# Attention turns: the weighted sums read in halves, one PSUM copy moved ahead of an exponential, weight rounding on another engine, and a new order at the end

## The chip, the cores and the metric

The kernel runs on one core of one Trainium2 chip. TensorE (PE) multiplies, VectorE (DVE), ScalarE (ACT) and GpSimd (POOL) work element by element, SyncE's queue (SP) issues most transfers. Each engine takes its instructions in the order in which the program wrote them for it; between engines, semaphores keep the order that the data need. The metric is the device time of one execution in microseconds, as the median of several runs.

## The reference

One encoder layer on 1024 positions of 1024 channels, in float32:

```
h = rms_norm(x, norm1_g);  z = h @ w_in
a, gate, q, k, v = split(z)
conv_out = silu(layer_norm(depthwise_conv(a * sigmoid(gate))))
q, k = rms_norm per head;  attn_out = neighbourhood_attention(q, k, v, rpb)
x = x + concat(conv_out, attn_out) @ w_out
h = rms_norm(x, norm2_g)
x = x + (silu(h @ w_gate) * (h @ w_up)) @ w_down
```

The attention has 8 heads of 64 channels on a grid of 16 rows by 64 columns. Each query sees a window of 8 rows by 16 columns, clamped inside the grid, with a learned bias per offset, a softmax over the window, and a weighted sum of the values. The change lies in this part and just behind it.

## The kernel before

Matrices are multiplied in two rounded parts: a value is rounded ("hi", `fp32r`), the rest ("lo") is the value minus hi, and `mac` adds three products (L122 to L126). `split` (L114) makes both parts: ScalarE casts, another engine subtracts.

The attention is cut into 8 sets, listed in `order` (L720): a half of the grid's rows (`rh`) by one of four column blocks (`cb`). A set has 128 queries and 253 to 372 keys; it has four pairs of heads. Index `i` counts all 32 pairs, `i // 4` is the set and `i % 4` the pair. For one pair:

- `score_mm(i)` (L732): TensorE makes the scores of two heads, each in a PSUM bank of its own.
- `score_max` (L746): VectorE adds the bias table, writes to SBUF tile `e`, and takes the maximum of each row. The table of a set comes by one large transfer (`table`, L668).
- `score_exp` (L761): ScalarE takes the exponential and its sum; `score_norm` (L770): VectorE inverts the sums, GpSimd scales `e`.
- `flip(i)` (L777): TensorE transposes the weights into two banks; `flip_out(i, r, eng)` (L787) copies bank `r` to SBUF, on ScalarE unless VectorE is named.
- `weigh(i)` (L795): TensorE multiplies the values with the weights and sums into `o`, one PSUM tile of 128x512 for each set, a quarter for each pair. There are two such tiles at a time.
- `evac_hi` (L817, ScalarE) and `evac_lo` (L822, VectorE) read the whole tile of a finished set as hi and lo parts.

The value rows that `weigh` reads come by `load_vw` (L693), eight or more small transfers for each column block, issued by SP. Each transfer signals on one of eight lanes, and a lane's next transfer is not issued before the last one has landed.

The PSUM banks come from three tags: `mm` with four, `tp` with two (`o` lies there), `cx` with two. Scores and flips of odd pairs take `mm`, of even pairs `cx`, in turn. So the scores of pair i (even) go to the two banks that the flip of pair i-2 filled in the turn before, and have to wait until both `flip_out`s have read them; the flip of i-2 in the same turn then takes the banks that the scores of i filled.

The order of the work is written out by hand: `manual_schedule` keeps it (L78). The loop at L964 makes one turn for two pairs, i = 4, 6, ... 30, and within a turn the steps of different pairs interleave: TensorE does scores of i+1, flip of i-3, scores of i, weighing of i-5 and i-4, flip of i-2. Turns 14 to 28 each also prepare a quarter of a weight tile of the output projection (`take_parts`, L173; one of `jobs` each turn): ScalarE casts 128x256, GpSimd subtracts.

Behind the loop (L997 to L1026) stands its end: the last flips and weighings, `fill` (first products of the output projection for the channels that are finished; its first call also loads ScalarE's square-root table), `sum_split` and `conv_mean`, the mean of the convolution channels as a product with ones. Then the projection runs.

Of the kernel before, what the change touches and what calls it, by code (L numbers as in the profile page):

```python
# [6 lines left out]
F32 = mybir.dt.float32  # L7
F32R = mybir.dt.float32r
AF = mybir.ActivationFunctionType
OP = mybir.AluOpType  # L10
# [61 lines left out]
def build(ctx, tc, a):  # L72
# [41 lines left out]
    def split(hi, lo, src, sub=(pool,), cast=True):  # L114
        if cast:
            act.copy(hi, src)  # L116
        n = src.shape[-1] // len(sub)
        for i, eng in enumerate(sub):
            sl = slice(i * n, (i + 1) * n)
            eng.tensor_tensor(*[w[..., sl] for w in (lo, src, hi.bitcast(F32))], OP.subtract)  # L120
# [22 lines left out]
    chunks, raws = [], {}  # L143
# [29 lines left out]
    def take_parts(jobs, n=4, sub=pool):  # L173
        i = pos[1]
        hi, lo = chunks[i][2]()
        w = 1024 // n
        if i == 0:
            dve.tensor_copy(hi[:, :w], raws[i][:, :w])

        def part(o):  # L180
            sl = slice(o, o + w)
            split(hi[:, sl], lo[:, sl], raws[i][:, sl], (sub,), i + o > 0)
            if o + w == 1024:
                raws.pop(i)
                issue()
        pos[1] += 1
        jobs.extend(lambda o=o: part(o) for o in range(0, 1024, w))
# [480 lines left out]
    def table(rh, ty):  # L668
        n = AR[rh] * NCOL[ty]
        src = tf[rh, ty].rearrange("j i h c -> (j i) (h c)")  # L670
        if rh == 0 and ty == 0:
            parts = [(G(f"tab{k}")[:, :4 * n], 4 * k) for k in range(2)]
        else:
            parts = [(H(f"tab{rh}{ty}")[:, :NH * n], 0)]
        heads = []
        for w, h0 in parts:
            nc.sync.dma_start(w, src[:, h0 * n:h0 * n + w.shape[-1]])
            heads += [w[:, o:o + n] for o in range(0, w.shape[-1], n)]
        return heads
# [13 lines left out]
    def load_vw(cb, *gs):  # L693
        c0, ncol = WIN[cb]
        if (cb, gs[0] // 2) not in vwt:
            vwt[cb, gs[0] // 2] = G(f"vw{cb}{gs[0]}").rearrange("p (g d) -> p g d", d=512)
        w = vwt[cb, gs[0] // 2]
        v4 = vd.rearrange("(g r c) d -> r c g d", r=4, c=GW)
        for r in range(4):
            value_rows(w, r * ncol, slice(gs[0] % 2, gs[-1] % 2 + 1), v4[r, c0:c0 + ncol, gs[0]:gs[-1] + 1, :], ncol)  # L700
        n = whole(4 * ncol)
        if n > 4 * ncol:
            nc.sync.dma_start(w[4 * ncol:n, gs[0] % 2:gs[-1] % 2 + 1, :], zd[:n - 4 * ncol, :len(gs), :])
        for g in gs:
            vw[cb, g] = w[:, g % 2, :]
# [59 lines left out]
    def both(i, s):  # L765
        for hh in range(2):
            score_max(i, hh, s)
            score_exp(i, hh)

    def score_norm(i):  # L770
        rs = sums.pop(i)
        dve.reciprocal(rs, rs)  # L772
        for hh in range(2):
            pool.tensor_scalar(es[i][:, hh], es[i][:, hh], rs[:, hh:hh + 1], 1.0, op0=OP.mult, op1=OP.mult)  # L774


    def flip(i):  # L777
        pp[i] = [(mm if i % 2 else cx)(f"p{i}{r}") for r in range(2)]
        gs = groups(i // 4)
        m = whole(gs[0].stop)  # L780
        for hh in range(2):
            for g, k in enumerate(gs):
                for r, pt in enumerate(pp[i]):
                    q, o = slice(r * 64, r * 64 + 64), (hh * len(gs) + g) * 64
                    pe.transpose(pt[:m, o:o + 64], et[i][q, hh, k.start:k.start + m], ident[q, q])  # L785

    def flip_out(i, r, eng=None):  # L787
        gs = groups(i // 4)
        m, n = whole(gs[0].stop), len(gs) * P
        w = et[i].rearrange("p h n -> p (h n)")[:m, :2 * n].rearrange("p (r n) -> p r n", r=2)  # L790
        v = w.rearrange("p r (h g q) -> p r h g q", h=2, q=64)
        pTs[i] = [v[:, :, h] for h in range(2)]
        (eng.tensor_copy if eng else act.copy)(w[:, r], pp[i][r][:m, :n])  # L793
# [19 lines left out]
    def at_of(s_):  # L813
        rh, cb = order[s_]
        return [w[:, :, cb * P:cb * P + P] for w in at[rh]]

    def evac_hi(s_):  # L817
        if not at:
            at.extend(half(f"at{h}") for h in range(2))
        act.copy(at_of(s_)[0], os_[s_])  # L820

    def evac_lo(s_):  # L822
        hi, lo = at_of(s_)
        dve.tensor_tensor(lo, os_[s_], hi.bitcast(F32), OP.subtract)

    def value(t):
        z = nat(2, t, mm if t < 6 else tp)
# [4 lines left out]
    def load_window(cb):  # L832
        load_vw(cb, 0, 1)
        load_vw(cb, 2, 3)
# [34 lines left out]
    flip_out(0, 1, dve)  # L869
    step()  # L870
    load_vw(0, 3)
    tab[1, 3] = table(1, 2)
    load_window(3)


    xd = dr.tile([KB, P, S], F32, name="xd")
# [21 lines left out]
    def conv_mean(h):  # L898
        cw["m", h] = tp(f"mr{h}")
        for n, w in enumerate(cr[:2]):  # L900
            pe.matmul(cw["m", h], cr[2], w[:, h * 512:(h + 1) * 512], start=n == 0, stop=n == 1)
# [23 lines left out]
    def conv_var(h):  # L925
        pt = tp(f"vs{h}")
        cw["v", h] = SM(f"cv{h}", 4)
        column_rstd(cw["v", h], pt, cw["s", h], DC)
# [35 lines left out]
    for i in range(4, 32, 2):  # L964
        if i == 4:
            tab[0, 1] = tab[0, 2] = table(0, 1)
        if i == 8:
            tab[1, 1] = tab[1, 2] = table(1, 1)
        if i in (8, 12):
            load_window(i // 6)  # L970
        if i in (14, 22):
            take_parts(jobs)
        sc = score_mm(i + 1)
        if i == 4:
            score_norm(3)
        else:
            flip(i - 3)
        sa = score_mm(i)
        flip_out(i - 3, 0)
        both(i + 1, sc)  # L980
        both(i, sa)
        flip_out(i - 3, 1, dve)
        score_norm(i + 1)
        if i > 4:
            weigh(i - 5)
        weigh(i - 4)
        flip(i - 2)
        flip_out(i - 2, 0)
        flip_out(i - 2, 1, dve)
        score_norm(i)  # L990
        if i % 4 == 0 and i > 4:
            evac_hi(i // 4 - 2)
        if i % 4 == 2 and i > 6:
            evac_lo(i // 4 - 2)
        if jobs:
            jobs.pop(0)()
    fill(0, 4, 5)  # L997
    sum_split(0)
    flip(29)
    flip_out(29, 0)  # L1000
    flip_out(29, 1)
    flip(30)
    flip_out(30, 0)
    flip_out(30, 1, dve)
    weigh(27)
    weigh(28)
    evac_hi(6)
    fill(0, 6, 7)
    flip(31)
    flip_out(31, 0)  # L1010
    flip_out(31, 1)
    evac_lo(6)
    sum_split(1)
    conv_mean(0)
    fill(1, 4, 5, 6, 7)
    conv_dev(0)

    cm += [half(f"cm{h}") for h in range(2)]
    slots = {0: lambda: ([weigh(i) for i in (29, 30, 31)], evac_hi(7), evac_lo(7)), 3: lambda: conv_var(0),
             4: lambda: (conv_mean(1), conv_dev(1)), 6: lambda: (conv_rows(0), conv_norm(0, 0)), 12: lambda: conv_var(1),  # L1020
             18: lambda: conv_rows(1),
             19: lambda: (act.activation(warm, eps, AF.Silu), [conv_norm(0, c) for c in (1, 2, 3)],
# [596 lines left out]
```

## Time and profile before

| What | Value |
|---|---|
| Median of 3 runs | 1013.18 us (1012.17 to 1014.35) |
| The profiled execution, its own time | 1013.09 us |
| Its span on the core | 1011.4 us |
| TensorE clock granted | 1.00 of full speed |
| TensorE busy | 1005.3 us (99%) |
| VectorE, ScalarE, GpSimd busy | 781.5, 477.6, 456.5 us |
| 230 to 287 us, the attention turns: TensorE, VectorE, ScalarE, GpSimd busy | 55.6, 45.2, 51.0, 39.8 us |
| 287 to 297 us, their end | 9.7, 5.8, 9.1, 5.6 us |

A row of the timeline gives the start in us from the span's start, the duration in us, the engine, the line, the operation, what is written from what is read (names of tiles, `o<-e,vw`), the shape, how many instructions were merged, and in brackets how long the engine sat idle before it and what ended that. TensorE records a float32 product as two instructions, so a weighing of two pairs is 24 rows, the scores of a pair are 4, and a flip is 12. The chain of waits goes back from the last instruction, at each step to what released it.

### The profile page before, as it was taken

To read this page: it belongs to the slowest core of one execution; us is meant where nothing else is said; L and a number is where in the kernel's file an instruction comes from. 1 tells how busy PE (TensorE), PEld (TensorE's weight loads), DVE (VectorE), ACT (ScalarE), POOL (GpSimd) and SP (SyncE) were. 2 spreads that over 40 slices of the span, in tenths; PEclk is the share of its full clock that TensorE was granted. 3 is DMA by queue.
4 is the path that set the end of the run, shared out by engine and by line. 5 is a ranking of instruction groups with operands and counts; after the bars stand their busy time and mean duration, and the time that the engine had idled before them with its cause. 6 is when DMAs were issued, how large, how long until landed. Compare 5 with 4: busy or idle time off the path is not lost.

```text
span 1011.4 us, 15446 instructions
## 1 busy us (share of the span) xinstructions
PE 1005.3 (99%) x5442; PEld 841.1 (83%) x5442; DVE 781.5 (77%) x1242; ACT 477.6 (47%) x1044; POOL 456.5 (45%) x385
## 2 busy tenths in 40 slices
PE   9999999999999999999999999999999999999998
PEld 7888888886788888888888888888888888888887
DVE  5788997896869376987877778778778766768874
ACT  7556357837987245532443333333433453443432
POOL 1036674535763375274655666566665100003300
PEclk9999999999999999999999999999999999999999
DMA  9416782235524520224343343433441796634631
GB/s 343 180 47 219 210 239 90 90 111 187 173 83 172 202 85 21 76 103 156 120 151 125 134 139 125 148 130 118 156 135 44 279 363 222 207 105 131 222 115 42
DMA packets 75757, 151.72 MB, mean 150 GB/s; under 512 B 14472, under 2 KB 23560, under 8 KB 75040
## 3 DMA queue, kind: packets, MB, share of 16 engines
q1 hardware_dynamic: 73664, 147.20, 43.1%
q10 hardware_dynamic: 2016, 3.54, 1.0%
q8 instruction: 43, 0.70, 0.3%
q14 instruction: 34, 0.28, 0.1%
HBM read 112.07 MB, written 44.11 MB: 154 GB/s over the span
## 4 chain that ended last, share of the span: by engine, by line
PE 93%; DVE 3%; DMA 2%; POOL 1%; ACT 0%; SPq 0%; issue 0%; DVEq 0%; ACTq 0%
PE B L124 6%; PE B L125 6%; PE B L126 6%; PE D L124 4%; PE D L125 4%; PE D L126 4%; PE pj L124 3%; PE z L125 3%; PE z L126 3%; PE pj L126 3%; PE pj L125 3%; PE gl L124 3%; PE gl L126 3%; PE gl L125 3%; PE z L124 3%; DVE cv L388 3%
## 5 line engine op out<-in xcount | busy, mean ns | idle before, releaser
L388 DVE SCALAR_TENSOR_TENSOR cv<-u,par,cv 128x1009 f32<-128x1009 f32 (+14 forms) x92 | 117.4, 1277 | 2.3
L1562 POOL TENSOR_TENSOR ou<-ou,resm 128x512 f32<-128x512 f32 x8 | 12.5, 1562 | 140.2 <-DVE ou L1553 126.5
L415 POOL TENSOR_TENSOR pa<-pa,pr 128x1022 f32<-128x1022 f32 (+5 forms) x24 | 58.0, 2418 | 38.1 <-ACT pr L414 37.6
L116 ACT CAST op<-sr 128x512 fp32r<-128x512 f32 x77 | 47.6, 619 | 56.8 <-PE B3d L126 26.4
L120 DVE TENSOR_TENSOR op<-sr,op 128x512 fp32r<-128x512 f32 x77 | 57.8, 751 | 17.0 <-ACT op L116 16.8
L116 ACT CAST op<-wd 128x512 fp32r<-128x512 f32 x54 | 33.4, 619 | 29.4 <-DVE wd L1457 18.3
L1110 DVE TENSOR_TENSOR ts<-gu,ts 128x512 f32<-128x512 f32 x36 | 40.5, 1126 | 0.6
L120 DVE TENSOR_TENSOR op<-wd,op 128x512 fp32r<-128x512 f32 x54 | 39.1, 724 | 2.4 <-ACT op L116 1.3
L774 POOL TENSOR_SCALAR e<-e,rs 128x341 f32<-128x341 f32 (+5 forms) x64 | 32.8, 528 | 17.2 <-DVE rs L772 14.8
L763 ACT ACTIVATE e<-e,mx 128x341 f32<-128x341 f32 (+5 forms) x64 | 34.9, 550 | 10.9 <-DVE mx L758 10.7
L1371 DVE TENSOR_TENSOR g<-D,g 128x512 f32<-128x512 f32 x22 | 15.2, 689 | 24.0 <-PE D L126 24.0
L442 ACT ACTIVATE sq<-z,r 128x64 f32<-128x64 f32 x96 | 28.3, 328 | 5.9 <-PE z L126 5.9
L758 DVE CUSTOM_DVE_ANT_0 e<-s,tab 128x341 f32<-128x341 f32 (+5 forms) x64 | 27.6, 479 | 3.4 <-PE s L741 3.0
L1348 ACT ACTIVATE D<-D 128x512 f32<-128x512 f32 x22 | 12.8, 582 | 36.5 <-DVE D L1347 36.5
L414 ACT ACTIVATE pr<-u,par 128x1022 f32<-128x1022 f32 (+5 forms) x24 | 27.0, 1138 | 1.6 <-ACT vs L472 1.6
L1064 POOL TENSOR_TENSOR sq<-sq,sq 128x512 f32<-128x512 f32 x12 | 17.6, 1464 | 16.5 <-ACT sq L1060 16.2
L741 PE MATMUL s<-kT,qT 64*128 64x341 f32 (+5 forms) x128 | 24.3, 458 | 0.4 <-ACT e L793 0.4
L806 PEld LDWEIGHTS o<-e,vw 128*64 128x64 f32 (+1 forms) x336 | 18.1, 136 | 6.4 <-issue 6.2
L806 PE MATMUL o<-e,vw 128*64 128x128 f32 (+1 forms) x336 | 21.9, 277 | 0.7 <-DMA vw<-vd 0.5
L793 DVE COPY e<-p 128x384 f32<-128x384 f32 (+2 forms) x30 | 16.1, 536 | 8.0 <-PE p L785 7.3
L1060 ACT ACTIVATE sq<-xT 128x512 f32<-128x512 f32 x16 | 10.0, 632 | 25.3 <-DVE xT L954 25.2
L954 DVE TENSOR_TENSOR xT<-pj,xT 128x512 f32<-128x512 f32 x16 | 10.7, 681 | 14.3 <-PE pj L126 14.3
(1502 smaller groups left out, 3785.9 us busy)
## 6 DMA issues: line engine op xcount, KB each, us to landing
gu<-in_gu SPq DMA_DIRECT2D x44, 512.0 KB
sr<-sd SPq DMA_DIRECT2D x77, 256.0 KB
sd<-sd SPq DMA_DIRECT2D x22, 512.0 KB
wd<-in_wd SPq DMA_DIRECT2D x36, 256.0 KB
sd<-g SPq DMA_DIRECT2D x33, 256.0 KB
x<-in_x SPq DMA_DIRECT2D x8, 512.0 KB
xT<-in_xp SPq DMA_DIRECT2D x8, 512.0 KB
xd<-xT SPq DMA_DIRECT2D x16, 256.0 KB
```

The source lines that it names most:

```text
L116: act.copy(hi, src)
L120: eng.tensor_tensor(*[w[..., sl] for w in (lo, src, hi.bitcast(F32))], OP.subtract)
L124: pe.matmul(acc, lh, rh, start=start, stop=False, skip_group_check=True)
L125: pe.matmul(acc, lh, rl, start=False, stop=False, skip_group_check=True)
L126: pe.matmul(acc, ll, rh, start=False, stop=stop, skip_group_check=True)
L388: dve.scalar_tensor_tensor(acc[:, o], uc[:, i], dwk[:, c, t:t + 1], acc[:, o], OP.mult, OP.add)
L415: pool.tensor_tensor(pa[:, o], pa[:, o], pr[:, o], OP.add)
L442: act.activation(sq[:, h * HD:(h + 1) * HD], z[:, h * HD:(h + 1) * HD], AF.Square, scale=r, accum_out=ss[:, h:h + 1])
L763: act.activation(e, e, AF.Exp, bias=mx.pop((i, hh)), scale=-1.0, accum_out=sums[i][:, hh:hh + 1])
L774: pool.tensor_scalar(es[i][:, hh], es[i][:, hh], rs[:, hh:hh + 1], 1.0, op0=OP.mult, op1=OP.mult)
L806: pe.matmul(os_[s_][hh * HD:(hh + 1) * HD, hp], v[:n, c:c + HD], pTs[i][hh][:n, :, g], start=g == 0, stop=g == len(gs) - 1)
L1110: (pool if (i, n) in ON_POOL else dve).tensor_tensor(o, l, r, OP.subtract)
```

## The change

- The finished sums are no longer read as a whole set. `evac` reads a slice of the pairs, and `evac_half(i)` reads the two pairs that end with pair i. In turn i the hi half of pairs up to i-5 is read at the turn's end, and the lo half of pairs up to i-7 ahead of the weighing.
- In the turn, `flip_out(i-2, 0)` now stands ahead of `score_exp(i, 1)` on ScalarE. `score_norm(i)` moves from the turn's end into the next turn, behind the first maximum.
- In `take_parts` with GpSimd, VectorE makes the hi part in place of ScalarE.
- The transfer of one bias table is issued between the two halves of a block's value rows, where it stood ahead of both.
- The end of the loop is written in another order: flip 29 first, then `fill`, the weighing of 27 and 28, flips 31 and 30, and `conv_mean(0)` ahead of the second `sum_split`.

```
@@ take_parts
         def part(o):
             sl = slice(o, o + w)
-            split(hi[:, sl], lo[:, sl], raws[i][:, sl], (sub,), i + o > 0)
+            if sub is pool:
+                dve.tensor_copy(hi[:, sl], raws[i][:, sl])
+            split(hi[:, sl], lo[:, sl], raws[i][:, sl], (sub,), sub is not pool and i + o > 0)
@@ reading of the sums
-    def evac_hi(s_):
+    def evac(s_, lo=False, ks=slice(0, 4)):
         if not at:
             at.extend(half(f"at{h}") for h in range(2))
-        act.copy(at_of(s_)[0], os_[s_])
-
-    def evac_lo(s_):
-        hi, lo = at_of(s_)
-        dve.tensor_tensor(lo, os_[s_], hi.bitcast(F32), OP.subtract)
+        h, l = [w[:, ks] for w in at_of(s_)]
+        if lo:
+            dve.tensor_tensor(l, os_[s_][:, ks], h.bitcast(F32), OP.subtract)
+        else:
+            act.copy(h, os_[s_][:, ks])
+
+    def evac_half(i, lo=False):
+        evac(i // 4, lo, slice(i % 4 - 1, i % 4 + 1))
@@ transfers ahead of the loop
     load_vw(0, 3)
+    load_vw(3, 0, 1)
     tab[1, 3] = table(1, 2)
-    load_window(3)
+    load_vw(3, 2, 3)
@@ a turn
         sc = score_mm(i + 1)
-        if i == 4:
-            score_norm(3)
-        else:
+        if i > 4:
             flip(i - 3)
         sa = score_mm(i)
         flip_out(i - 3, 0)
-        both(i + 1, sc)
-        both(i, sa)
+        score_max(i + 1, 0, sc)
+        score_norm(i - 2 if i > 4 else 3)
+        score_max(i + 1, 1, sc)
+        score_exp(i + 1, 0)
+        score_exp(i + 1, 1)
+        score_max(i, 0, sa)
+        score_max(i, 1, sa)
+        score_exp(i, 0)
         flip_out(i - 3, 1, dve)
         score_norm(i + 1)
+        if i > 6:
+            evac_half(i - 7, True)
+        if jobs:
+            jobs.pop(0)()
         if i > 4:
             weigh(i - 5)
         weigh(i - 4)
         flip(i - 2)
         flip_out(i - 2, 0)
         flip_out(i - 2, 1, dve)
-        score_norm(i)
-        if i % 4 == 0 and i > 4:
-            evac_hi(i // 4 - 2)
-        if i % 4 == 2 and i > 6:
-            evac_lo(i // 4 - 2)
-        if jobs:
-            jobs.pop(0)()
+        score_exp(i, 1)
+        if i > 4:
+            evac_half(i - 5)
@@ behind the loop
+    flip(29)
+    flip_out(29, 0)
+    score_norm(30)
+    evac_half(25, True)
+    flip_out(29, 1, dve)
     fill(0, 4, 5)
     sum_split(0)
-    flip(29)
-    flip_out(29, 0)
-    flip_out(29, 1)
-    flip(30)
-    flip_out(30, 0)
-    flip_out(30, 1, dve)
     weigh(27)
     weigh(28)
-    evac_hi(6)
+    evac_half(27)
+    evac_half(27, True)
+    for i in (31, 30):
+        flip(i)
+        flip_out(i, 0)
+        flip_out(i, 1, dve)
     fill(0, 6, 7)
-    flip(31)
-    flip_out(31, 0)
-    flip_out(31, 1)
-    evac_lo(6)
+    conv_mean(0)
     sum_split(1)
-    conv_mean(0)
     fill(1, 4, 5, 6, 7)
     conv_dev(0)
...
-    slots = {0: lambda: ([weigh(i) for i in (29, 30, 31)], evac_hi(7), evac_lo(7)), 3: lambda: conv_var(0),
+    slots = {0: lambda: ([weigh(i) for i in (29, 30, 31)], evac(7), evac(7, True)), 3: lambda: conv_var(0),
```

## The prediction, on record before the changed kernel was run

> **What bounds the kernel now.** First the head of the page, for the span; TensorE is busy throughout, and its clock is granted in full (both in the table above).
>
> ```profile
> span 1011.4 us, 15446 instructions
> ```
>
> A busy TensorE says little here, because the ends of matmuls are modelled and touch; what counts is how far apart the starts lie. The change touches the attention turns (about 236 to 286 us) and the tail behind them (to 297). Behind that TensorE runs projections back to back, so I let a shift at 297 pass to the end in full. So I read next the chain of waits in that stage, then TensorE's timeline in its early and middle turns.
>
> ```profile
> 240.81 5.36 DMA tab<-tf
> 246.18 5.60 DMA vw<-vd
> ```
>
> ```profile
> 237.96 0.73 PE L785 MATMUL p<-ident,e 64*128 64x64 f32 x8 [0.31 <-DVE mx L758]
> ...
> 239.83 0.73 PE L741 MATMUL s<-kT,qT 64*128 64x276 f32 x4 [0.37 <-ACT e L793]
> ...
> 250.06 1.31 PE L806 MATMUL o<-e,vw 96*64 96x128 f32 x20
> 251.92 0.44 PE L806 MATMUL o<-e,vw 96*64 96x128 f32 x4 [0.55 <-DMA vw<-vd]
> 252.29 0.54 PE L785 MATMUL p<-ident,e 64*96 64x64 f32 x12
> ...
> 255.72 0.54 PE L785 MATMUL p<-ident,e 64*96 64x64 f32 x12
> ...
> 256.72 0.50 PE L785 MATMUL p<-ident,e 64*96 64x64 f32 x12
> 257.06 0.79 PE L741 MATMUL s<-kT,qT 64*128 64x341 f32 x4
> 257.78 1.53 PE L806 MATMUL o<-e,vw 96*64 96x128 f32 x24
> 259.24 0.69 PE L785 MATMUL p<-ident,e 64*96 64x64 f32 x12
> ...
> 263.14 0.59 PE L785 MATMUL p<-ident,e 64*128 64x64 f32 x12
> ...
> 265.52 1.89 PE L806 MATMUL o<-e,vw 96*64 96x128 f32 x24
> 267.34 0.59 PE L785 MATMUL p<-ident,e 64*128 64x64 f32 x12
> ```
>
> The early turns end on transfers: the table of 1152 KB, then the value rows behind it, for which the weighing at 250.06 stands still. Undisturbed, 24 products take 257.78 to 259.24, 1.46; here 252.29 - 250.06 = 2.23, so 0.77 is lost. At 265.52 it is 1.82, so 0.36 is lost.
>
> Now one late turn (i = 28, rows 372 wide) on three engines, by their timelines.
>
> ```profile
> 278.53 0.58 PE L785 MATMUL p<-ident,e 64*128 64x64 f32 x12
> 278.95 0.84 PE L741 MATMUL s<-kT,qT 64*128 64x372 f32 x4
> 279.63 0.54 PE L785 MATMUL p<-ident,e 64*128 64x64 f32 x12
> 280.08 0.90 PE L741 MATMUL s<-kT,qT 64*128 64x372 f32 x4
> 280.90 1.53 PE L806 MATMUL o<-e,vw 128*64 128x128 f32 x24
> 282.37 0.59 PE L785 MATMUL p<-ident,e 64*128 64x64 f32 x12
> ...
> 286.19 0.59 PE L785 MATMUL p<-ident,e 64*128 64x64 f32 x12
> ```
>
> ```profile
> 279.55 0.47 ACT L793 COPY e<-p 128x384 f32<-128x384 f32 x1
> 279.91 0.42 ACT L116 CAST wo06h<-wo06r 128x256 fp32r<-128x256 f32 x1
> ...
> 281.02 0.60 ACT L763 ACTIVATE e<-e,mx 128x372 f32<-128x372 f32 x1 [0.32 <-DVE mx L758]
> ```
>
> ```profile
> 279.80 0.67 DVE L824 TENSOR_TENSOR at<-o,at 128x512 fp32r<-128x512 f32 x1
> ...
> 281.31 0.54 DVE L758 CUSTOM_DVE_ANT_0 e<-s,tab 128x372 f32<-128x372 f32 x1
> ...
> 281.77 0.54 DVE L758 CUSTOM_DVE_ANT_0 e<-s,tab 128x372 f32<-128x372 f32 x1
> ...
> 282.24 0.55 DVE L793 COPY e<-p 128x384 f32<-128x384 f32 x1
> 282.71 0.15 DVE L772 RECIPROCAL rs<-rs 128x2 f32<-128x2 f32 x1
> ```
>
> A turn on TensorE is: scores of i+1, flip of i-3, scores of i, weighing of i-5 and i-4, flip of i-2. From flip to flip this one takes 282.37 - 278.53 = 3.84. The scores at 280.08 start when ScalarE's copy (279.55 + 0.47 = 280.02) has emptied their bank: flip to scores is 0.45 here and 0.34 at 256.72. Scores to weighing is 0.82, of which about 0.05 is the restart. So the floor of this turn is near 3.84 - 0.11 - 0.05 = 3.68; at 341 columns a turn without waits took 259.24 - 255.72 = 3.52. ScalarE waits in its turn for VectorE's maximum, which stood behind the reading of the sums at 279.80.
>
> **The change, part by part.**
>
> *Copy ahead of the last exponential.*
>
> ```profile
> 274.67 0.69 PE L785 MATMUL p<-ident,e 64*128 64x64 f32 x12
> ```
>
> The bank is emptied one exponential (0.60) earlier, and the wait of the scores goes. ScalarE now holds exp(i,1) until the flip is done; behind it stand the half reading and the next turn's first copy, which have the 0.3 that it idles before 281.02. The normalising of i-2 (two scalings on GpSimd) moves behind that exponential into the next turn, ahead of the other normalising and the subtraction on that queue, and must be done before the flip there, some 3.5 later; its reciprocal makes VectorE wait some 0.2 early in a turn, hidden under the scores. Against the floors the turns of before lose: i=18 (263.14 - 259.24 = 3.90 against 3.52) 0.38; i=20 (267.34 - 263.14 = 4.20, less the 0.36 of the transfer) 0.16; i=26 (278.53 - 274.67 = 3.86 against 3.52 and some 0.06 for the longer flips) 0.28; i=28 0.16; i=30 (3.82) 0.14; i=6 its wait of 0.37 at 239.83, of which I keep 0.3. Sum 1.4 gained at most; nothing at least.
>
> *Weight rounding on VectorE.* Eight casts of 128x256 leave ScalarE (0.42 each) and stand on VectorE. The nearest row there is twice as wide:
>
> ```profile
> L178 DVE CAST wkq<-wk0r x1: 427/427/427, 4.5 to 4.5; 128x512 fp32r<-128x512 f32 x1
> ```
>
> So 0.2 to 0.43 each; I take 0.25. It stands behind the half reading and ahead of a copy that waits for the flip anyway, so it costs nothing; without that cover it would be 8 x 0.25 = 2.0. GpSimd's subtraction keeps its place and waits for this cast.
>
> *Table between value rows.* Four of the eight transfers of value rows now pass the table on SP's queue. Last of all is still the value rows' second half; its bytes ahead are the same, but the queue can move the small pieces while the table's descriptors start. I give it 1.0 (0 to 1.5). The table comes up to 2.8 later (half of the 5.6 that the rows took after it), at 246.2 + 2.8 = 249.0; its first reader, the maximum of i=13, stands in the turn whose weighing is at 250.06, and under the forecast that turn comes some 1.5 later. So it costs nothing; if the turn came on time, a few tenths.
>
> *Sums read out by halves.* This is where I see the price. Each set of four pairs sums into one 128x512 PSUM tile; before, it was read whole after its last product. Now pairs 0 and 1 are read first, and in turns i = 8, 12, 16, 20, 24, 28 VectorE's reading of that half (of i-7) is written ahead of the weighing of i-5, which writes pair 3 of the **same tile**. Six times, then, a reader stands between two writers of one tile. Is TensorE held until it is through? No row of before shows this case. The lower bound is 0, if different columns are let through. What the rows do show is that TensorE never writes a bank under a reader: at 237.96 it waits for VectorE, at 239.83 for ScalarE, at 280.08 it starts 0.06 behind the copy's end. I take it that the guard covers the tile, and so take the wait.
>
> On this the Trainium skill, page "PSUM — Partial Sum Buffer", section "PSUM bank collisions raise a hardware error", speaks against the change: TensorE's write and another engine's read of one bank and the same partitions must not meet, even at different columns, and it advises to guard by bank. By that rule the wait stands; no run yet shows it.
>
> The price, at 372 columns: VectorE comes to the reading in order. The scores end at 280.08 + 0.90 = 280.98. Then come maximum (281.77 - 281.31 = 0.46), maximum (282.24 - 281.77 = 0.47), copy (282.71 - 282.24 = 0.47), reciprocal (0.1) and the half. The half is 0.33 (half of 0.67) to 0.67; nearer the first, because most of a row goes by its columns, with a start-up that doesn't halve: 0.40. With two hand-overs of some 0.05 that is 2.0 behind 280.98, while the weighing started 0.08 ahead of it: **2.1 lost**. Queued behind it on TensorE are both weighings and the flip, for which ScalarE's copy and exp(i,1) wait, so the whole turn shifts. ScalarE, too, reads in two halves what it read at once, one start-up more, inside its idle 0.3.
>
> ```profile
> L758 DVE CUSTOM_DVE_ANT_0 e<-s,tab x64: 401/478/547, 225.8 to 285.3; 128x341 f32<-128x341 f32 x16, 128x372 f32<-128x372 f32 x16, 128x253 f32<-128x253 f32 x8, 128x276 f32<-128x276 f32 x8
> ```
>
> Maxima range from 0.40 to 0.55, so two of them shorten the narrow turns by up to 0.3: 2 x 2.1 (i=20, 28) + 2 x 2.0 (16, 24) + 2 x 1.85 (8, 12) = **11.9**. Under it the transfer waits vanish: TensorE comes later than they land (0.77 + 0.36 = 1.1 gained).
>
> *Other end.* The flips of 30 and 31 no longer stand ahead of the weighing.
>
> ```profile
> 287.62 1.62 PE L785 MATMUL p<-ident,e 64*128 64x64 f32 x24
> 289.18 1.53 PE L806 MATMUL o<-e,vw 128*64 128x128 f32 x24
> ...
> 292.50 0.39 PE L901 MATMUL mr<-crl,onesr 128*128 128x512 f32 x1
> ```
>
> ```profile
> 287.75 1.28 ACT L959 ACT_TABLE_LOAD   x1
> ...
> 289.16 0.60 ACT L116 CAST crh<-cs 128x512 fp32r<-128x512 f32 x1
> ```
>
> ```profile
> 289.84 1.27 POOL L120 TENSOR_TENSOR crl<-cs,crh 128x512 fp32r<-128x512 f32 x1 [1.05 <-ACT crh L116]
> ```
>
> 24 flips took 1.56 where 2 x 0.42 suffice: 0.7 lost on norms, and that goes. But ScalarE's table load moves behind a half reading and a copy, some 0.8 later than the 287.75 - 286.19 = 1.56 behind the last flip, and the rounding of the column sums and GpSimd's subtraction follow it: 2.35 + 1.41 (287.75 to 289.16) + 0.6 + 1.27 and hand-overs, some 5.9 behind the flip, against 292.50 - 286.19 = 6.3 before. I take 0.4 gained (-0.5 to 0.7).
>
> **Sum.** 11.9 - 1.4 - 1.1 - 0.4 = +9.0. The profiled execution lasted 1013.09 (span 1011.4 and 1.7 around it), 0.1 under the median of 1013.18: 1013.1 + 9.0 = **1022.1**.
>
> **The rivals.**
>
> *A: the halves are guarded apart.* Then nothing is paid, and the turns reach their floors. For it: the two parts share no column; against it: every guard seen covers a whole tile. The weighing at 265.52 stays tied to transfers, so up to there the gain is 1.0 to 1.2, of 1.9 offered (0.3 + 0.38 + 0.16 + 1.1). Then 0.28 + 0.16 + 0.14 of the late turns, and 0.6 in the tail: 2.3, so **1010.8**.
>
> *B: the same, with the queue no faster and the tail's load in the way.* Value rows land when they did; only the late turns gain: **1012.5**.
>
> *C: the wait, and VectorE full besides.* In a 372 turn VectorE would hold four maxima (1.87), two copies (0.94), two reciprocals with their wait (0.4), half reading (0.3) and cast (0.25): 3.76 against the floor of 3.68. If the cast costs 0.43 and the reciprocals wait 0.4, each of eight turns pays 0.4: **1025.3**. It decides once VectorE's sum passes the turn of TensorE.
>
> **How the numbers follow.** Forecast 0.81, A 0.09, B 0.04, C 0.06: tile-wide guards in every row seen make the wait likely, not certain, and C needs two costs at their ends. The forecast's own range is 1019.5 to 1024.5 (half reading 0.33 to 0.67: -0.4 to +1.6; narrow turns and gains about 1.5 either way). With C and the upper slack, 1018.5 to 1025 holds some 8 in 10; A and B lie outside. A measurement of this kernel tells about 0.2%, 2.0 us, from no change. Faster by that: two thirds of A, 0.06. Same: the rest of A, and B: 0.07. Slower: 0.87.
>
> **What would show it.** Right: in six turns the weighing's rows name VectorE's reading of the sums as releaser, with 1.8 to 2.2 between scores' end and weighing; turns alternate between about 5.8 and 3.6; no wait on value rows; the scores of i no longer wait for ScalarE. Wrong: all turns near 3.6 with the reading under the weighing (A), or turns without the wait above 3.8 (C).

## The result and the profile after

The changed kernel takes 1028.64 us (median of 4 runs, 1027.53 to 1030.72) against 1013.26 in the same session: a ratio of 1.0154, 95% interval 1.0132 to 1.0176. It is slower, as forecast, but by 15.4 where 9.0 stood in the forecast. The profiled execution took 1027.6, with a span of 1025.9: 14.5 more than the profiled one of before.

First TensorE's own waits between 225 and 311 us (what it waited for: us in total, times, the longest), then the row of the costliest groups for the weighing.

```profile
PE o L808 <- DVE at L824: 12.0, 7, 2.0
```

```profile
L808 PE MATMUL o<-e,vw 128*64 128x128 f32 (+1 forms) x336 | 25.1, 303 | 10.2 <-DVE at L824 10.2
```

The weighing now waits 12.0 for VectorE's reading of the sums, and the transfers have gone from the list. Its products also got longer: 303 ns in the mean, where the same group of before had 277. The timeline of TensorE shows both.

```profile
245.01 0.66 PE L808 MATMUL o<-e,vwf 128*64 128x128 f32 x8 [1.82 <-DVE at L824]
...
254.02 2.46 PE L808 MATMUL o<-e,vw 96*64 96x128 f32 x24 [1.86 <-DVE at L824]
...
264.53 2.72 PE L808 MATMUL o<-e,vw 96*64 96x128 f32 x24 [1.95 <-DVE at L824]
267.18 0.88 PE L787 MATMUL p<-ident,e 64*96 64x64 f32 x12
...
271.12 0.59 PE L787 MATMUL p<-ident,e 64*128 64x64 f32 x12
...
275.41 1.53 PE L808 MATMUL o<-e,vw 96*64 96x128 f32 x24 [1.97 <-DVE at L824]
276.87 0.59 PE L787 MATMUL p<-ident,e 64*128 64x64 f32 x12
...
279.12 1.54 PE L808 MATMUL o<-e,vw 128*64 128x128 f32 x24
280.59 0.59 PE L787 MATMUL p<-ident,e 64*128 64x64 f32 x12
...
284.96 2.67 PE L808 MATMUL o<-e,vw 128*64 128x128 f32 x24 [1.81 <-DVE at L824]
287.57 0.91 PE L787 MATMUL p<-ident,e 64*128 64x64 f32 x12
...
295.89 1.53 PE L808 MATMUL o<-e,vw 128*64 128x128 f32 x24 [1.95 <-DVE at L824]
...
301.06 0.96 PE L787 MATMUL p<-ident,e 64*128 64x64 f32 x24
...
309.49 2.19 PE L808 MATMUL o<-e,vw 128*64 128x128 f32 x36
```

Six weighings are held, every second turn, in the places that the forecast named: 1.82 + 1.86 + 1.95 + 1.97 + 1.81 + 1.95 = 11.4. The turns in between are the control: VectorE's order is the same there, but it reads another tile than the weighing writes, and the weighing (279.12) has no wait. So the guard is on the tile, and on the whole of it: the two touch different columns. (The tile fills one PSUM bank; no run here tells a guard by tile from one by bank.) The seventh wait, 0.66, is the same pattern at the end, where `evac_half(25, True)` stands ahead of `weigh(27)`; the forecast counted six. ScalarE's hi reading of the same half stands between the same two writers too, but a turn earlier, and no weighing waits for it.

But three of the six are followed by products at half speed: 24 of them take 2.46, 2.72 and 2.67 where 1.53 is usual, and the flips behind them 0.88 and 0.91 where 0.54 (shape `64*96`) and 0.59 (`64*128`) are usual. The view by stretches of time shows why. Its columns here are: stretch, length, then busy time (and instructions) of PE, PEld, DVE, ACT and POOL, the granted clock, the share of the DMA engines and GB/s.

```profile
251.04:254.45 3.41, 1.55 (x26) 1.09 (x24) 2.89 (x13) 2.89 (x11) 1.74 (x5) 1.00 1.03 419
254.45:257.86 3.41, 3.41 (x38) 2.94 (x34) 0.43 (x1) 0.48 (x2) 0.37 (x1) 0.50 1.01 313
261.28:264.69 3.41, 1.46 (x22) 0.75 (x20) 3.40 (x14) 3.12 (x11) 2.76 (x7) 1.00 0.44 116
264.69:268.10 3.41, 3.41 (x38) 3.08 (x38) 0.00 (x0) 0.00 (x0) 1.63 (x4) 0.50 0.50 135
271.52:274.93 3.41, 1.92 (x28) 1.03 (x22) 3.33 (x14) 3.13 (x10) 2.97 (x7) 1.00 0.43 106
274.93:278.34 3.41, 2.93 (x52) 2.47 (x54) 1.64 (x6) 1.11 (x4) 1.89 (x4) 1.00 0.89 293
281.76:285.17 3.41, 1.60 (x22) 1.00 (x20) 3.41 (x15) 2.91 (x10) 2.94 (x7) 1.00 0.03 7
285.17:288.58 3.41, 3.41 (x38) 3.08 (x36) 0.21 (x1) 0.02 (x1) 1.40 (x4) 0.50 0.00 0
```

In three stretches TensorE is granted half its clock. The clock records of the trace put them at 254.45, 264.69 and 285.17, each 3.41 long, and 3 and 9 times 3.41 from the first: the fall comes on a fixed grid. In the stretch of the grid just ahead of each, TensorE was busy 1.55, 1.46 and 1.60 of 3.41. Where it was busy 1.92 (271.52 to 274.93, a pause of 1.97 cut in two by the grid) the clock stayed. A stretch at half clock can lose at most half of 3.41, 1.7. None of this stood in the forecast.

### The profile page after: what moved, and what is told of

Read it like the earlier page. It is cut to its first block, busy times and chain, and to the rows that moved or that the text cites. A ratio compares the mean times of both kernels' runs of the same rounds, so it can differ in the third digit from the quotient of the medians.

```text
span 1025.9 us, 15443 instructions
## 1 busy us (share of the span) xinstructions
PE 1008.9 (98%) x5442; PEld 844.9 (82%) x5442; DVE 786.6 (77%) x1259; ACT 475.0 (46%) x1041; POOL 457.8 (45%) x385
## 4 chain that ended last, share of the span: by engine, by line
PE 94%; DVE 2%; DMA 2%; ACT 1%; issue 0%; SPq 0%; POOL 0%; ACTq 0%; DVEq 0%
PE B L124 6%; PE B L125 6%; PE B L126 6%; PE D L124 4%; PE D L125 4%; PE D L126 4%; PE z L124 4%; PE z L126 4%; PE z L125 4%; PE gl L124 3%; PE pj L124 3%; PE gl L126 3%; PE gl L125 3%; PE pj L126 3%; PE pj L125 3%; PE o L808 2%
## 5 line engine op out<-in xcount | busy, mean ns | idle before, releaser
L808 PE MATMUL o<-e,vw 128*64 128x128 f32 (+1 forms) x336 | 25.1, 303 | 10.2 <-DVE at L824 10.2
L808 PEld LDWEIGHTS o<-e,vw 128*64 128x64 f32 (+1 forms) x336 | 20.9, 151 | 16.5 <-DVE at L824 13.1
L795 ACT COPY e<-p 128x384 f32<-128x384 f32 (+2 forms) x32 | 14.8, 466 | 21.4 <-PE p L787 20.9
```

The costliest lines, as they stand in the source:

```text
L808: pe.matmul(os_[s_][hh * HD:(hh + 1) * HD, hp], v[:n, c:c + HD], pTs[i][hh][:n, :, g], start=g == 0, stop=g == len(gs) - 1)
```

## The experiments

Theory after the result: the loss is, first, TensorE held by a reader that stands between two writers of one tile (11.4), and second, the half clock that follows the pause (up to 1.7 for each of the pauses that meet the grid badly). Rivals: VectorE is full; the half clock has another cause or costs nothing; the loss lies in the rounding, the table or the end.

**The lo half behind the copy.**

```
@@ a turn
-        if i > 6:
-            evac_half(i - 7, True)
         if jobs:
...
         flip_out(i - 2, 1, dve)
+        if i > 6:
+            evac_half(i - 7, True)
         score_exp(i, 1)
```

> Kernel after, with one line moved: VectorE's lo half of a set (of i-7) is written behind the copy of the flip of i-2, and no longer ahead of the weighing, so that no reader of a tile stands between two writers of it. Theory (held writer, and a half clock that follows the idle): the 12.0 us of waits of the weighing on VectorE's reading go, and with them the three stretches at half clock (about 1.7 us lost in each, 5.1 together): 1028.6 - 12.0 - 5.1 = 1011.5 (1010 to 1013), clock 1.00 throughout. Rival VectorE full: the rounding of 128x256 took 0.48 to 0.56 there and not 0.25, so a wide turn holds about 4 x 0.47 + 2 x 0.47 + 0.2 + 0.32 + 0.5 = 3.85 of VectorE against 3.68 of TensorE; if that decides, eight turns pay 0.2 or more each: 1013 to 1016, with TensorE waiting for VectorE's maxima or copies. Rival that the loss lies in the rounding, the table or the end: stays near 1028.

Measured: 1012.55 (10 runs, 1010.85 to 1015.71), ratio to before 0.9998 (0.9986 to 1.001). The trace of the profiled run holds no clock records, but in the turns every weighing of 24 products without a wait takes 1.53 or 1.54, as at full clock. One moved line takes 16 us away: the whole loss. VectorE isn't full: the last turn, from flip to flip in the timeline of TensorE below, is 285.64 - 281.93 = 3.71, against the floor of 3.68 that was estimated. The fall of the clock goes with the pauses. What is left are two waits for value rows, 0.88 and 0.46, and the 0.66 of the end, where the line was not moved.

```profile
252.04 0.44 PE L808 MATMUL o<-e,vw 96*64 96x128 f32 x4 [0.88 <-DMA vw<-vd]
...
266.91 0.44 PE L808 MATMUL o<-e,vw 96*64 96x128 f32 x4 [0.46 <-DMA vw<-vd]
267.28 0.59 PE L787 MATMUL p<-ident,e 64*128 64x64 f32 x12
...
281.93 0.59 PE L787 MATMUL p<-ident,e 64*128 64x64 f32 x12
...
285.64 0.96 PE L787 MATMUL p<-ident,e 64*128 64x64 f32 x24
...
294.06 2.19 PE L808 MATMUL o<-e,vw 128*64 128x128 f32 x36
```

**The lo half first in the turn.** The same line, put ahead of `score_max(i + 1, 0, sc)`.

> Kernel after, with the lo half (of i-7) written at the head of VectorE's turn, ahead of the first maximum. The reader still stands between two writers of one tile, but some 1.6 us earlier than in the kernel after. Theory (a wait until the reader is through, priced by the reader's place): no wait on the reading is left at the weighing, or a few tenths; VectorE instead waits at its head for ScalarE's hi half (copy 0.5, exponential 0.55, half 0.35 behind the flip, some 0.5 later than the scores are there) and its reading delays the maxima by up to 0.8 in a turn: 1011.5 to 1018, no stretch at half clock. Rival, a fixed price for each alternation of writers and reader, wherever it stands: six waits near 2 us stay, 1026 to 1030.

Measured: 1017.5 (4 runs, 1017.1 to 1017.9), ratio 1.0045 (1.003 to 1.006). TensorE's waits in this kernel, from 230 to 300 us:

```profile
PE o L808 <- DVE at L824: 1.8, 5, 0.6
PE p L787 <- DVE mx L760: 1.5, 6, 0.4
```

The reader still stands between the same two writers, and in the turns it holds the weighings 1.2 in all and not 11.4 (0.6 of the 1.8 is the wait at the end). So it isn't the alternation that is dear, but how late the reader comes on its engine. Here the price moved: the maxima behind the reading come later, flips wait 1.5, and the later turns take 4.1 to 4.4 each, held ones and those between alike, where 3.5 to 3.7 is usual. VectorE stands idle at their head until ScalarE's hi half is there (VectorE's timeline):

```profile
279.89 0.42 DVE L824 TENSOR_TENSOR at<-o,at 128x256 fp32r<-128x256 f32 x1 [0.72 <-ACT at L826]
```

**TensorE kept busy while it is held.** In turns 8, 12, ... 28, n products into the new set's tile, which is overwritten later:

```
+    def keep_busy(s_, n):
+        w = tp(f"o{s_}")
+        for _ in range(n):
+            pe.matmul(w, ident, kT[:, 0, :512], start=True, stop=True)
+        os_[s_] = w.rearrange("p (c q) -> p c q", c=4)
@@ a turn
         if i > 4:
+            if i % 4 == 0:
+                keep_busy(i // 4 - 1, 3)
             weigh(i - 5)
```

> Kernel after, with three products that nothing needs (128x128 with 128x512, float32, into the new set's own tile, overwritten later) written between the scores of i and the weighing of i-5 in each turn i = 8, 12, ... 28, so that TensorE works while it would be held. Each takes some 0.58 (the scores' 0.42 for 372 columns), 1.74 together, of the 1.8 to 2.0 that the weighing is held. Theory (the half clock follows TensorE's idle): the turns stay as long as the reading makes them, but the three stretches at half clock go: 1028.6 - 5.1 = 1023.5 (1022.5 to 1025), clock 1.00. Rival (the clock falls for another reason, or its fall costs nothing because VectorE sets the turn): 1028 or more, the three added products costing up to 0.3.

Measured: 1027.49 (1026.65 to 1027.67), clock 1.00. The clock stayed full, but the time hardly fell and missed the expected range. The run can't tell theory from rival, because the added products were mis-sized. From its timeline:

```profile
251.82 2.84 PE L814 MATMUL o<-kT,ident 128*128 128x512 f32 x6
```

Three take 2.84, and the weighing starts 2.78 behind their start (at 254.60), 0.8 to 1.0 more than the holds of 1.81 to 1.97. So two, and in another run a single one of 256 columns:

> Kernel after with two added products of 128x512 in each of the six held turns instead of three. The three took 2.84 in the trace, 0.92 each and not the 0.58 estimated, so they ended 0.8 to 0.9 behind the point to which the weighing is held anyway, six times, about 5 in all: that run could not tell the theories apart. Two take about 1.85, as long as the weighing is held (1.81 to 1.97). Theory (half clock follows TensorE's idle, and costs half of each 3.41 us stretch): clock 1.00, turns otherwise as in the kernel after, 1028.6 - 3 x 1.7 = 1023.5 (1022.5 to 1024.5). Rival (the clock's fall costs little, since VectorE sets the length of the turns): 1027 to 1028.6 although the clock is 1.00.

> Kernel after with one added product of 128x256 (about 0.46) at the head of each of the six held turns: TensorE then idles 1.35 to 1.5 in each instead of 1.81 to 1.97. In the kernel after, the half clock came where TensorE idled 1.85 or more within a stretch of 3.41 of a fixed grid, and not where it idled 1.53 or less. Theory with that threshold (about half of a stretch): clock 1.00 and 1023.5 (1022.5 to 1024.5), the same as with two full products. Rival (any pause above a microsecond brings the half clock): three or more stretches at half clock stay, 1027 to 1029.

Measured: 1022.32 (1022.2 to 1022.65) with two, 1022.63 (1022.36 to 1022.79) with the short one, both at clock 1.00, ratios 1.0093 and 1.0095. From the timeline, first the two products, then the weighing behind the short one:

```profile
251.58 1.98 PE L814 MATMUL o<-kT,ident 128*128 128x512 f32 x4
```

```profile
253.90 1.53 PE L808 MATMUL o<-e,vw 96*64 96x128 f32 x24 [1.23 <-DVE at L830]
```

With useless work in the pause the kernel gets 6.3 faster (1028.64 - 1022.32; 5.2 between the profiled spans, 1025.9 and 1020.7), though the turns are as long as the reading makes them. The half clock follows the pause, and has a price of its own. Its size can be read from flip to flip: the turns take 301.06 - 238.03 = 63.03 in the changed kernel and 295.90 - 237.48 = 58.42 with two products in each pause. That is 4.6, or 1.5 for each of the three stretches; the other 0.55 lies ahead of the turns, where the two kernels do not differ. The short product shows that a pause of 1.2 to 1.3 doesn't bring it. The rival, that any pause above a microsecond does, falls.

**The halves alone**, on the kernel before: `evac` by halves in the places of the change, the rest as before.

```
         score_norm(i + 1)
+        if i > 6:
+            evac_half(i - 7, True)
         if i > 4:
             weigh(i - 5)
...
-        if i % 4 == 0 and i > 4:
-            evac_hi(i // 4 - 2)
-        if i % 4 == 2 and i > 6:
-            evac_lo(i // 4 - 2)
+        if i > 4:
+            evac_half(i - 5)
```

> Kernel before, with the reading by halves alone: hi half of i-5 at the turn's end, lo half of i-7 ahead of the weighing, everything else (place of the copy, rounding on ScalarE, table, end) as before. Theory: the whole loss comes from this part: six weighings held 1.7 to 2.1 (about 11.5), two to five stretches at half clock (1.7 each), less up to 1.1 of transfer waits: 1013.2 + 14 to 19 = 1027 to 1032. Rival (the half clock needs the other edits too, or the loss lies in them): 1015 to 1024.

Measured: 1028.69 (1027.37 to 1028.85), ratio 1.0153, mean clock 0.993 in the profiled run. TensorE's waits, and four stretches of the clock's grid:

```profile
PE o L806 <- DVE at L822: 11.2, 6, 2.0
```

```profile
250.75:254.16 3.41, 1.70 (x30) 1.24 (x28) 2.75 (x13) 2.98 (x11) 1.74 (x4) 1.00 0.97 357
254.16:257.57 3.41, 3.41 (x36) 2.65 (x34) 0.63 (x2) 0.75 (x2) 0.19 (x1) 0.50 1.03 422
...
271.23:274.64 3.41, 1.70 (x20) 0.81 (x18) 3.27 (x13) 3.41 (x13) 2.57 (x8) 1.00 0.34 96
274.64:278.05 3.41, 3.15 (x54) 2.68 (x56) 1.16 (x4) 1.49 (x6) 1.34 (x3) 1.00 0.71 233
```

This part alone brings a loss as large as the whole change, with the same two terms. That the two times agree so closely is partly chance: the clock records show four stretches at half clock here and three in the changed kernel. The lines also show that the busy time alone does not decide: TensorE was busy 1.70 in the stretch from 250.75 and in that from 271.23, and the clock fell behind the first and stayed behind the second.

**The table ahead of both halves of the rows**, on the kernel with the lo half behind the copy.

> The kernel with the lo half behind the flip's copy (1012.55), with the bias table issued ahead of both halves of the value rows again, as before. In the trace with the new order the last value rows landed at 251.90 and the weighing started again at 252.04, against 251.78 and 251.92 before: the bytes ahead of them are the same. Theory (order of issue changes nothing here): 1012.5, within 0.5. Rival (the new order brings the rows forward 1.0, as first argued): 1013.3 to 1013.7. Opposite rival (the new order holds the maxima of i=13, whose table landed at 249.77 and not at 246.17): 1011.5 to 1012.

Measured: 1012.27 (11 runs, 1010.9 to 1014.86), ratio to before 0.9994 (0.9985 to 1.0003): the order makes no difference that can be seen. The chain of waits of the kernel with the changed order has this piece (start, us):

```profile
244.13 7.77 DMA vw<-vd
```

It ends at 251.90; before, 246.18 + 5.60 = 251.78. The last of the rows lands no earlier. The profiled run of this variant happened to show the second cause by itself, in a kernel whose weighings in the turns wait for no reading. Timeline and stretches:

```profile
268.02 0.47 PE L808 MATMUL o<-e,vw 96*64 96x128 f32 x4 [2.49 <-DMA vw<-vd]
268.42 0.90 PE L787 MATMUL p<-ident,e 64*128 64x64 f32 x12
```

```profile
264.89:268.30 3.41, 0.92 (x16) 0.63 (x12) 1.34 (x7) 1.21 (x5) 2.33 (x6) 1.00 0.46 132
268.30:271.71 3.41, 3.41 (x34) 2.45 (x32) 1.89 (x7) 1.71 (x5) 0.27 (x1) 0.50 0.48 138
```

Here a late transfer made the pause (busy 0.92 of 3.41), and the half clock followed just the same. The turn from the flip at 268.42 took 5.23 where the same turn takes 3.71 with the changed order: again 1.5 lost.

**The copy ahead alone**, on the kernel before. It took three runs, since the first had a fault of its own. All three hold this edit (the turn of the change without the halves):

```
-        both(i + 1, sc)
-        both(i, sa)
+        score_max(i + 1, 0, sc)
+        score_norm(i - 2 if i > 4 else 3)
+        score_max(i + 1, 1, sc)
+        score_exp(i + 1, 0)
+        score_exp(i + 1, 1)
+        score_max(i, 0, sa)
+        score_max(i, 1, sa)
+        score_exp(i, 0)
...
-        score_norm(i)
+        score_exp(i, 1)
```

> Kernel before with the copy ahead of the last exponential alone (and the normalising of i-2 moved with it into the next turn): sums read as whole sets as before, rounding on ScalarE, table and end as before. By the losses of single turns against their floors this gains 1.4 at most: 1011.8 (1011.5 to 1013). Rival (ScalarE, 95% busy in the turns with the rounding still on it, is the bound as soon as the copy stands ahead): no gain or a loss, 1013 to 1015.

> Kernel before with the copy ahead of the last exponential alone, as in the run before, but with the normalising of pair 30 ahead of the fills at the end. There it stood behind the rounding of the column sums on GpSimd's queue, and the flip of 30 waited 3.7 for it: that was this variant's own fault and no property of the edit. What was left of that run's loss lay in the turns: flips waited 0.2 to 0.35 for GpSimd's scalings, which stood behind a subtraction that waits for ScalarE's rounding. Theory (the copy ahead needs the rounding off ScalarE): the turns lose about 0.8 against before, the end nothing: 1013.8 (1013.3 to 1015). Rival (the step gains by itself, as first argued): 1011.6 to 1012.5.

> The run of the copy alone, with the weight part's job (rounding on ScalarE, subtraction on GpSimd) written ahead of the weighing, where the kernel after has it, and no longer at the turn's end. At the turn's end its subtraction stood on GpSimd's queue ahead of both scalings of the next turn and held them 0.86 for ScalarE's rounding. Theory (the copy ahead gains only if the subtraction stands behind the scalings, on whichever engine the rounding is): the flips no longer wait for scalings in the turns, which lose no more 0.8 and gain some 0.5 against before; of the 3.0 by which the copy alone was slower, 1.3 goes in the turns, and what is lost at the end (flip 30 waiting 0.67 for its scaling, written late) stays: 1013 to 1014.5. Rival (the whole readings do not fit beside the copy): 1015 or more.

Measured: 1020.83 (5 runs, 1019.56 to 1021.71) with the scaling of pair 30 behind the rounding of the column sums, where a flip waited 3.7 for it and the clock stood at half for 6.83 (two stretches of the grid); 1015.56 (7 runs, 1015.15 to 1016.94), ratio 1.0033 (1.0022 to 1.0044), with that mended; 1013.28 (11 runs, 1012.37 to 1014.92), ratio 1.0004 (0.9995 to 1.0013), with the job moved ahead of the weighing. The first two lie above both ranges expected for them, the third is in its range. From the second of them, GpSimd and TensorE by their timelines:

```profile
269.73 0.73 POOL L120 TENSOR_TENSOR wo04l<-wo04r,wo04h 128x256 fp32r<-128x256 f32 x1 [0.86 <-ACT wo04h L116]
...
270.48 1.12 POOL L774 TENSOR_SCALAR e<-e,rs 128x372 f32<-128x372 f32 x2
```

```profile
271.11 0.40 PE L785 MATMUL p<-ident,e 64*128 64x64 f32 x6 [0.17 <-POOL e L774]
```

The subtraction waits 0.86 for ScalarE's rounding with both scalings of the next turn behind it on the queue, and the flips wait for these. With the job ahead of the weighing no flip in the turns waits. What is left is at the end, where the flip of 30 waits 0.66 for a scaling that this variant writes late. In the profiled execution of this last run the turns take 285.87 - 238.20 = 47.67 from flip to flip, against 286.19 - 237.96 = 48.23 before: 0.56 gained, and as much lost at the end. So alone the step loses, and beside a change in GpSimd's queue it gains a little in the turns of one trace; a gain in the time of the whole kernel was not measured.

**Rounding on ScalarE again**, on the kernel with the lo half behind the copy.

```
-            if sub is pool:
-                dve.tensor_copy(hi[:, sl], raws[i][:, sl])
-            split(hi[:, sl], lo[:, sl], raws[i][:, sl], (sub,), sub is not pool and i + o > 0)
+            split(hi[:, sl], lo[:, sl], raws[i][:, sl], (sub,), i + o > 0)
```

> The kernel with the lo half behind the flip's copy (1012.55), with the rounding of the weight parts on ScalarE again; its place, ahead of the weighing, stays. ScalarE then has 8 casts of some 0.35 more, between the exponential of i and the copy of the flip of i-2, and its busy time in the turns goes from 30.4 of 33.6 to about 33. Theory (ScalarE full: the rounding on VectorE is what lets the other edits gain): the eight turns that carry a cast lose 0.2 to 0.4 each: 1014 to 1016. Rival (ScalarE has room once the copy stands ahead): 1012.5, within 0.5.

Measured: 1012.09 (11 runs, 1010.55 to 1014.84), ratio to before 0.9993 (0.9984 to 1.0002). The theory that ScalarE is full falls; which engine rounds makes no difference that can be seen. It was the job's new place, not its engine, that the copy needed.

**The rows earlier.** For a kernel that beats both, the two waits for value rows were tried.

```
-    load_vw(3, 0, 1)
     tab[1, 3] = table(1, 2)
-    load_vw(3, 2, 3)
+    load_vw(3, 0, 1)
+    load_vw(3, 2)
+    load_vw(3, 3)
...
+            load_vw(1, 0, 1)
             tab[1, 1] = tab[1, 2] = table(1, 1)
-        if i in (8, 12):
-            load_window(i // 6)
+            load_vw(1, 2, 3)
+        if i == 12:
+            load_window(2)
```

> The kernel with the lo half behind the flip's copy, with transfers in another order: the bias table first, then the value rows of block 3 by groups 0 and 1, group 2, group 3 (the weighing that stood 0.88 needs no group 3), and the first half of block 1's rows ahead of the large table of that block instead of behind it. Theory (what is left of waits in this kernel, 0.88 and 0.46, is the order of bytes, and once in the trace a wait of 2.49 for the same rows brought a stretch at half clock): both waits shrink to 0.4 or less together, and the scatter of the times with them: 1011.3 (1010.5 to 1012). Rival (the rows are bound by bandwidth whatever their order, or the table now comes late for its maxima): 1012.3 to 1014.

Measured: 1012.64 (11 runs, 1011.24 to 1015.76), ratio 1.0004 (0.9995 to 1.0013). No gain. The first wait is gone, and the second has taken up the time (TensorE's timeline):

```profile
265.99 0.44 PE L808 MATMUL o<-e,vw 96*64 96x128 f32 x4 [0.84 <-DMA vw<-vd]
266.68 0.96 PE L787 MATMUL p<-ident,e 64*128 64x64 f32 x12 [0.24 <-DVE mx L760]
```

Counted from the first flip of the turns (237.29 here, 237.73 with the changed order, 237.96 before), the flip behind that weighing starts at 29.39, 29.55 and 29.38. The turn of that weighing had started 0.85 earlier than with the changed order (24.30 against 25.15): what was gained ahead of the transfer is mostly given back there. No version measured beats the kernel before by more than can be told from no change.

## Why the prediction was right about the sign and wrong about the size

The profiled executions differ by 14.5. The terms: held weighings +11.4, half clock +4.6 (the 63.03 against 58.42 above), end -0.4, everything else -1.1 (what is left of the sum); forecast were +11.9, nothing, -0.4 and -2.5. The forecast missed the profiled difference by 5.5: 4.6 for the clock and 1.4 for gains that were smaller, less 0.5 for holds that were shorter.

**The step that failed** is the price of a held turn. It counted the pause (2.1 for 372 columns) and then let the rest of the turn shift at its usual speed: the "Queued behind it on TensorE are both weighings and the flip" was read as a delay only. The runs show that a pause of 1.7 or more can leave TensorE at half clock for 3.41, another 1.5 lost. That term, missing, is 4.6 in the profiled runs. The medians missed by 6.5, and 6.3 of it goes when the pause is filled; two of the four runs of the changed kernel took 2 to 3 us more than the profiled one, one of them at a lower mean clock (0.991), the other at the same (0.995), and what that other one lost was not traced. With TensorE kept busy in the pause the kernel took 1022.3 and 1022.6, and 1022.1 was predicted. That it comes so near is in part luck: the holds were 0.5 smaller than forecast and the gains 1.4 smaller, errors that go opposite ways.

On this the Trainium skill, page "TensorE: Matmul & The Clock Gate", section "HAM oscillation — how this bites in real kernels", has the mechanism: TensorE's clock falls to half when it idles. It puts the limit at gaps of more than some 3.4 us, by which none of the six holds would have counted. The traces disagree: pauses of 1.71 (the halves alone) to 2.49 were enough. That page's section "Part 1: The HAM clock gate (the "warmup" mystery)" gives a window of 3413 ns that runs freely, and there the traces agree: stretches of 3.41 on a grid.

**Halves, the wait.** Right in mechanism, place and size: 11.4 against 11.9. VectorE's timeline in the last held turn has the chain as it was added up:

```profile
293.95 0.55 DVE L760 CUSTOM_DVE_ANT_0 e<-s,tab 128x372 f32<-128x372 f32 x1
...
294.42 0.54 DVE L760 CUSTOM_DVE_ANT_0 e<-s,tab 128x372 f32<-128x372 f32 x1
...
294.89 0.55 DVE L795 COPY e<-p 128x384 f32<-128x384 f32 x1
295.36 0.15 DVE L774 RECIPROCAL rs<-rs 128x2 f32<-128x2 f32 x1
295.43 0.40 DVE L824 TENSOR_TENSOR at<-o,at 128x256 fp32r<-128x256 f32 x1
```

Two maxima, copy, reciprocal, and the half in 0.40, as estimated; the weighing follows at 295.89. The turns alternate as said where the clock stayed: 276.87 - 271.12 = 5.75, then 280.59 - 276.87 = 3.72. With the half clock the pair is 287.57 - 280.59 = 6.98 and about 4.0.

**Copy ahead.** 0.58 was expected of the last three turns (0.28, 0.16 and 0.14). With the lo half out of the way these and the two turns before them, from the flip at 267.28 to that at 285.64, took 18.36, against 286.19 - 267.34 = 18.85: 0.5. That kernel holds the other edits too; with the copy and the job's move alone the last three turns took 3.71, 3.71 and 3.86 (3.86, 3.84 and 3.82 before), 0.24 gained. Up to about 267 nothing was gained, because the transfers set that part. That the step needs the job's move was not seen: "ahead of the other normalising and the subtraction on that queue" is right, but only because the job moves from the turn's end to the weighing. The forecast took "GpSimd's subtraction keeps its place" for granted; with the job left where it was, the subtraction would have come ahead of both scalings.

**Weight rounding** cost nothing, as said. **Table:** wrong that the rows come 1.0 earlier: with either order the last of them landed at 251.8 to 251.9. The transfer waits went from the changed kernel only because TensorE came later, and are back (0.88 and 0.46) as soon as the wait is taken out. **End:** from the last flip of the loop to the weighing of the last three pairs it takes 309.49 - 301.06 = 8.43; before, with the row below, 294.98 - 286.19 = 8.79. That is 0.36 gained, 0.4 forecast, with the seventh wait of 0.66 inside it. The second product of the column means starts 306.99 - 301.06 = 5.93 behind the last flip, as the working said (5.9, against 6.3 before).

```profile
294.98 2.19 PE L806 MATMUL o<-e,vw 128*64 128x128 f32 x36
```

**Rivals.** A and B had no wait, and six waits are there. With the wait removed, 1012.55 was measured, near B's 1012.5 (the transfers come no earlier, as B has it). C falls: the turns without a wait, where the clock stayed, take 3.71 and 3.72, not above 3.8. Two slips in the working did not decide anything: C's own 1025.3 lies just outside the range that is said to hold it, and A takes 0.6 for the tail where the forecast takes 0.4, without a reason.

## What to carry to other kernels

Before a reader is written between two writers of one PSUM tile, look where it stands on its own engine: TensorE is held until everything ahead of it there is done, and moving one line (here, behind the next copy) makes the whole difference. Price a pause of TensorE twice: its length, and, when it leaves TensorE idle for about half of a 3.4 us stretch or more, some 1.5 more for the clock. When a step gains in one engine's order, read the other queues at the place that it leaves and the place that it takes: the same copy lost 3 us with a subtraction ahead of the scalings, and none with it behind.

## What was not expected of the hardware

The clock fell to half after pauses of 1.7 to 2.5 that left TensorE busy 0.92 to 1.70 of a stretch of 3.41 on the grid (27 to 50%), and once, with the start of the pause of 3.7 in the stretch, after 1.86 (54%). It stayed after 1.92 and 1.94 (271.52 and 292.00 in the changed kernel, 56 and 57%), but also after 1.70 in the halves alone. So near half the busy time, as the profile counts it, does not decide alone, and what does is open. Whether a pause counts depends on how it lies on the grid, and so changes from run to run: of the runs of the changed kernel, three had a mean clock of 0.995 and one, the slowest, 0.991. The kernel with the lo half behind the copy scatters from 1010.85 to 1015.71, and its three slowest runs are those with a mean clock of 0.998. It is likely, but was not traced run by run, that a late transfer made the pause there, as in the one profile that shows it.

VectorE's rounding of 128x256 took 0.27 or 0.56. In the changed kernel the five slow ones start beside GpSimd's scaling, here by the timelines of VectorE and GpSimd:

```profile
284.83 0.56 DVE L183 CAST wo06h<-wo06r 128x256 fp32r<-128x256 f32 x1
```

```profile
284.68 1.11 POOL L776 TENSOR_SCALAR e<-e,rs 128x341 f32<-128x341 f32 x2 [0.47 <-DVE rs L774]
```

The three quick ones there start beside a scaling too, and then it was the scaling that took longer: two of them took 1.29 at 341 columns, where 1.08 is usual. In the kernel with the lo half behind the copy, where the rounding starts ahead of the scaling, all eight took 0.27. The overlap is seen, its part in the 0.56 was not tested, and it cost nothing here.
